# Seven products for eight moved from the down projection to gate and up, in five feed-forward stages

## The chip, the core and the metric
The kernel runs on one core of a Trainium2 chip. A core has TensorE (PE in the profile, its weight loads are PEld), VectorE (DVE), ScalarE (ACT), GpSimd (POOL) and SyncE (SP), which issues the DMAs. Each engine takes its instructions in a fixed order; engines wait for each other through semaphores. The metric is the device time of one execution in microseconds; lower is better.

## What is computed
512 tokens of width 1024 pass through two blocks: a first layer (a state-space mixer beside chunked attention) and four more layers (stick-breaking, differential and convolution mixers). Each of the five layers ends in the same feed-forward stage, which is all that the change touches:

```
h2 = rmsnorm(x, norm_ffn_g[l])
x = x + (jax.nn.silu(h2 @ w_gate[l]) * (h2 @ w_up[l])) @ w_down[l]
```

The hidden width is 2816, which is 22 tiles of 128. Everything is float32.

## The kernel before
Activations lie transposed: `self.x[k]` (k = 0 to 7) holds 128 features by 512 tokens. A float32 product is made of three matmuls in a shorter format: an operand is split by `hilo` (L369, L371) into a high part (ACT copies with rounding) and a low part (DVE subtracts); then hi·hi, hi·lo and lo·hi are added in PSUM (L321, L323, L325). `xh` and `xl` are the parts of the activation times the norm's gain; the norm's factor per token, the tile `bc`, is multiplied in after the product. Weights come by DMA as `raw` tiles of up to eight 128x128 tiles and are split on the way.

The class `Kern` first writes a plan: a list of units (one output tile, up to four k-tiles: 12 matmuls of 512 columns) and of sevenths. `execute` walks the plan; at each item it issues loads, sums and splits two units ahead, then the unit's matmuls, then what follows from the finished product. Generators such as the norm's run a step per item (`tick`). A scheduler below puts the instructions of each engine in their final order by its own forecast of durations.

A group is a block product with four quarters on each side, done by seven products of half the width instead of eight (the Winograd form): GpSimd adds the weights to four sums (L255), the right sides need differences of activations, and the seven results (L272 to L276, matmuls of 256 columns) are added into the output quarters (`take`, L287). Before, gate and up are plain units (`pair`, L526 to L580), and `w_down` is done by groups for 18 of the 22 hidden tiles, in three parts between the units of gate and up; `halves` makes the right sides from the hidden tiles (L637). The last four hidden tiles are plain units at the stage's end. A hidden tile is silu(gate·bc)·bc times up: a multiplication on DVE (L526), silu on ACT (L560), a multiplication on GpSimd (L561), one on DVE (L576).

A PSUM bank of the sevenths comes from `bank`: five rotating "a" banks, or three "z" banks in the layers whose mixers keep them apart.

## Time and profile before

| | us |
|---|---|
| median of 3 runs | 3128.26 |
| lowest, highest | 3126.29, 3129.25 |
| the profiled execution | 3124.52 |
| its span, first to last instruction | 3122.7 |
| PE busy / DVE / ACT / POOL | 3054.8 / 2174.7 / 1502.7 / 1173.0 |

The profile is one execution. A row by line and shape gives the tile written, the tiles read, the form, how often, the busy time, the mean time of one, and how long its engine stood idle just before, with what ended that. A row in time gives the start, the length, the engine, the work. A matmul lasts longer than its step: the next one starts before it ends, so the step between starts is what counts. A stretch counts every instruction that touches it. The five feed-forward stages lie at about 336 to 695, 959 to 1293, 1573 to 1906, 2137 to 2472 and 2756 to 3111 us.

### The profile page before, as it was taken

What the parts mean: (1) busy time and instruction counts of PE and PEld (TensorE: products, weight loads), DVE (VectorE), ACT (ScalarE), POOL (GpSimd) and SP (SyncE); (2) the same over time, 40 slices, a digit from 0 to 9 for tenths busy, and PEclk for the clock granted to TensorE, in tenths of its full rate; (3) what the DMA queues carried; (4) which work ended last, traced back from release to release, by engine and by line L of the source; (5) the groups of instructions that cost most, each with busy time, mean ns of one, the idle gap of its engine ahead of it and who ended that gap; (6) DMA issues with size and microseconds to landing.
All of it is one profiled execution on the core that took longest, in us unless ns stands there. A gap on an engine that the chain in (4) does not pass through costs nothing.

```text
span 3122.7 us, 44415 instructions
## 1 busy us (share of the span) xinstructions
PE 3054.8 (98%) x16236; PEld 2624.9 (84%) x16236; DVE 2174.7 (70%) x3541; ACT 1502.7 (48%) x2793; POOL 1173.0 (38%) x997
## 2 busy tenths in 40 slices
PE   7799999999999999999999999999999999999998
PEld 6687788888887888888878888887888888878887
DVE  8887667677756776766657767655776777567765
ACT  5365444456754444555434435324343567544444
POOL 2731454452314544311145542114444322144543
PEclk9899999999999999999999999999999999999999
DMA  7332333322223333322233332233333322233332
GB/s 240 85 100 78 102 97 92 108 87 68 65 66 120 97 93 106 97 73 73 71 118 102 97 94 93 87 92 118 97 94 101 92 75 62 70 120 92 96 109 66
DMA packets 108203, 295.90 MB, mean 95 GB/s; under 512 B 23216, under 2 KB 27312, under 8 KB 107952
## 3 DMA queue, kind: packets, MB, share of 16 engines
q1 hardware_dynamic: 107984, 293.06, 31.2%
q8 instruction: 128, 2.10, 0.3%
q14 instruction: 91, 0.75, 0.1%
HBM read 286.46 MB, written 6.55 MB: 94 GB/s over the span
## 4 chain that ended last, share of the span: by engine, by line
PE 92%; DVE 4%; POOL 1%; issue 1%; ACT 1%; DMA 1%; SPq 0%; DVEq 0%; POOLq 0%; ACTq 0%
PE g L321 22%; PE g L325 22%; PE g L323 22%; PE a L276 3%; PE a L274 3%; PE a L272 3%; PE z L276 2%; PE z L274 2%; PE z L272 2%; DVE lo L371 1%; PE z L905 1%; PE a L360 1%; PE a L361 1%; DVE x L542 1%; PE a L359 1%
## 5 line engine op out<-in xcount | busy, mean ns | idle before, releaser
L371 DVE TENSOR_TENSOR lo<-raw,hi 128x512 fp32r<-128x512 f32 (+3 forms) x1075 | 862.6, 804 | 335.5 <-ACT hi L369 316.4
L321 PE MATMUL g<-xh,hi 128*128 128x512 f32 x2720 | 1069.7, 393 | 11.7 <-ACT hi L369 7.8
L369 ACT ACTIVATE hi<-raw 128x512 fp32r<-128x512 f32 (+3 forms) x1075 | 638.6, 596 | 903.2 <-PE g L323 694.4
L323 PE MATMUL g<-xl,hi 128*128 128x512 f32 x2720 | 1066.2, 392 | 0.5 <-DVE xl L401 0.5
L325 PE MATMUL g<-xh,lo 128*128 128x512 f32 x2720 | 1062.7, 392 | 0.9 <-DVE lo L371 0.9
L321 PEld LDWEIGHTS g<-xh,hi 128*128 128x128 f32 x2720 | 513.6, 189 | 112.4 <-ACT hi L369 7.8
L325 PEld LDWEIGHTS g<-xh,lo 128*128 128x128 f32 x2720 | 512.4, 188 | 107.4 <-DVE lo L371 1.5
L323 PEld LDWEIGHTS g<-xl,hi 128*128 128x128 f32 x2720 | 513.3, 189 | 97.2 <-DVE xl L401 0.9
L561 POOL TENSOR_TENSOR t<-t,bc 128x512 f32<-128x512 f32 x110 | 151.5, 1379 | 417.4 <-ACT t L560 417.4
L369 ACT ACTIVATE hi<-w 128x384 fp32r<-128x384 f32 x240 | 125.8, 524 | 243.3 <-PE g L323 189.2
L637 POOL TENSOR_TENSOR h<-h 128x256 f32<-128x256 f32 x180 | 177.1, 984 | 162.4 <-DVE h L576 156.9
L371 DVE TENSOR_TENSOR lo<-w,hi 128x384 fp32r<-128x384 f32 x240 | 189.4, 789 | 49.3 <-ACT hi L369 47.9
L421 POOL TENSOR_TENSOR acc<-acc,t 128x512 f32<-128x512 f32 x82 | 117.4, 1438 | 265.3 <-ACT t L420 245.1
L274 PE MATMUL a<-hl,hi 128*128 128x256 f32 x756 | 213.2, 283 | 0.0
L272 PE MATMUL a<-hh,hi 128*128 128x256 f32 x756 | 212.7, 282 | 0.0
L276 PE MATMUL a<-hh,lo 128*128 128x256 f32 x756 | 211.5, 283 | 0.0
L255 POOL TENSOR_TENSOR w<-raw 128x384 f32<-128x384 f32 x120 | 138.1, 1153 | 175.1 <-DMA raw<-in_weights_dram 123.6
L287 POOL TENSOR_TENSOR x<-x,u 128x512 f32<-128x512 f32 x120 | 154.6, 1307 | 111.6 <-DVE u L287 111.6
L526 DVE TENSOR_TENSOR t<-g,bc 128x512 f32<-128x512 f32 x182 | 124.5, 685 | 100.6 <-PE g L325 92.3
L371 DVE TENSOR_TENSOR hl<-h,hh 128x1024 fp32r<-128x1024 f32 x90 | 101.6, 1146 | 69.3 <-ACT hh L369 69.3
L272 PEld LDWEIGHTS a<-hh,hi 128*128 128x128 f32 x756 | 144.6, 191 | 4.5
L274 PEld LDWEIGHTS a<-hl,hi 128*128 128x128 f32 x756 | 144.7, 191 | 4.3
(382 smaller groups left out, 5225.3 us busy)
## 6 DMA issues: line engine op xcount, KB each, us to landing
raw<-in_weights_dram SPq DMA_DIRECT2D x388, 512.0 KB, 3.5
raw<-in_weights_dram SPq DMA_DIRECT2D x131, 384.0 KB, 3.4
raw<-in_weights_dram SPq DMA_DIRECT2D x50, 256.0 KB, 2.7
x<-in_xT_dram SPq DMA_DIRECT2D x16, 256.0 KB, 4.1
raw<-in_weights_dram SPq DMA_DIRECT2D x6, 448.0 KB, 3.3
x<-in_att_bias_dram SPq DMA_DIRECT2D x8, 256.0 KB, 6.0
kv<-kv SPq DMA_DIRECT2D x32, 64.0 KB, 2.3
out_dram<-x SPq DMA_DIRECT2D x8, 256.0 KB, 2.7
```

The costliest lines, as they stand in the source:

```text
L255: nc.gpsimd.tensor_tensor(out=src[out], in0=src[x], in1=src[y], op=ALU.add)
L272: nc.tensor.matmul(out=u.ps, lhsT=wh, rhs=xh, start=i == 0, stop=False)
L274: nc.tensor.matmul(out=u.ps, lhsT=wh, rhs=xl, start=False, stop=False)
L276: nc.tensor.matmul(out=u.ps, lhsT=wl, rhs=xh, start=False, stop=i == len(g.kps) - 1)
L287: eng.tensor_tensor(out=c, in0=c, in1=t, op=op)
L321: nc.tensor.matmul(out=out, lhsT=wh, rhs=xh, start=u.first and i == 0, stop=False)
L323: nc.tensor.matmul(out=out, lhsT=wh, rhs=xl, start=False, stop=False)
L325: nc.tensor.matmul(out=out, lhsT=wl, rhs=xh, start=False, stop=u.last and i == len(u.ks) - 1)
L369: nc.scalar.activation(out=hi, in_=src, func=ACTF.Copy)
L371: eng.tensor_tensor(out=lo, in0=src, in1=hi.bitcast(F32), op=ALU.subtract)
L561: nc.gpsimd.tensor_tensor(out=tg, in0=tg, in1=self.bc(n), op=ALU.mult)
L637: self.nc.gpsimd.tensor_tensor(out=h[:, out], in0=h[:, x], in1=h[:, y], op=op)
```

## The change
Gate and up go by groups, `w_down` by plain units. The first two hidden tiles (`pair(0)`, `pair(1)`) stay plain for gate and up; the other 20 are ten tile pairs, each with a gate group and an up group whose inner dimension is all eight k-tiles (seven products of four k-tile pairs: 84 matmuls of 256 columns). The right sides, differences of the scaled activations, are the same for all twenty groups of a stage; `rights_gen` makes them once at its start: two scaled copies on ACT, one difference on GpSimd, two on DVE, then both parts, for each of four k-tile pairs. Weight parts are split in tiles of 1024 columns (two products at once) with two buffers. The norm, silu and product work on tile pairs of 1024 columns (`gate_got`, `up_got`). The eight plain `w_down` units of each part are set among the groups of the next, after the second and the sixth product of a group; every one adds into `x` (L606 in the new file, L542 before). The stage ends in 16 plain units for the last six hidden tiles. GpSimd's sums and the scaled copies are held in program order against the scheduler.

```diff
 NFF = FF // P
-FF_PARTS = (6, 6, 6, 4)
+FF_PARTS = ((0, 1), (2, 3), (4, 5), (6, 7), (8, 9, 10))
 HALF = T // 2
-SEVEN = ("11", "w3", "w2", "12", "w1", "22", "w4")
+SEVEN = (("11", "11"), ("12", "21"), ("w2", 2), ("w3", 1), ("22", 3), ("w1", 0), ("w4", "22"))
 SUMS_AHEAD = 6
+DOWN_AHEAD = 8
+DOWN_BUFS = 1
+SEVEN_BUFS = 2
 MEM = 256
...
+                    fill(downs[di], self.p_ffn.tile([P, 4 * P], F32, tag="raw", name="raw", bufs=DOWN_BUFS))
+                    di += 1
+                while gi < len(groups) and groups[gi].first <= ui + SUMS_AHEAD and (
+                    (gi < 2 or groups[gi - 2].begun == 5) and (gi < 1 or groups[gi - 1].begun >= 2)
+                ) and all(c.raw is not None for c in groups[gi].chunks):
                     self.sums(groups[gi])
...
-        g.src = src
+        nc, n = self.nc, 4 * P
+        c1, c2 = (c.raw for c in g.chunks)
+        t = [self.p_ffn.tile([P, 2 * n], F32, tag=f"w{i}", name="w", bufs=1 + i) for i in range(2)]
+        (w2, w3), (w1, w4) = ((x[:, :n], x[:, n:]) for x in t)
+        for out, x, y in ((w1, c2[:, :n], c2[:, n:]), (w2, c1[:, :n], w1), (w3, c1[:, :n], c2[:, :n]),
+                          (w4, c1[:, n:], w2)):
+            self.tc.keep_in_program_order(nc.gpsimd.tensor_tensor(out=out, in0=x, in1=y, op=ALU.add))
+        for c in g.chunks:
+            c.left -= 1
+        g.src = {0: c1, 2: t[0], 5: t[1], 4: c2[:, n:]}
...
+        g, n = u.group, 4 * P
+        if u.i not in g.src:
+            u.hi, u.lo = g.next
+            return
+        if u.i == 4:
+            u.hi = self.p_hi.tile([P, n], F32R, tag="hi", name="hi")
+            u.lo = self.p_hi.tile([P, n], F32R, tag="lo", name="lo")
+            self.hilo(u.hi, u.lo, g.src[4])
+        else:
+            hi = self.p_ffn.tile([P, 2 * n], F32R, tag="wh", name="wh", bufs=SEVEN_BUFS)
+            lo = self.p_ffn.tile([P, 2 * n], F32R, tag="wl", name="wl", bufs=SEVEN_BUFS)
+            self.hilo(hi, lo, g.src[u.i])
+            u.hi, u.lo = hi[:, :n], lo[:, :n]
+            g.next = hi[:, n:], lo[:, n:]
+            g.begun = u.i
+        if u.i in (0, 4):
+            g.chunks[u.i == 4].left -= 1
...
+            g.ps = self.bank(self.drawn, [P, 2, HALF])
+        ps = g.ps[:, u.i % 2]
+        for kp in range(KD // 2):
+            wh, wl = u.hi[:, kp * P:(kp + 1) * P], u.lo[:, kp * P:(kp + 1) * P]
+            xh, xl = g.rights(kp, SEVEN[u.i][1])
+            nc.tensor.matmul(out=ps, lhsT=wh, rhs=xh, start=kp == 0, stop=False)
             self.tick(self.fine)
...
+        def tt(out, x, y, op=ALU.add):
+            nc.vector.tensor_tensor(out=out, in0=x, in1=y, op=op)
+        if u.i == 1:
+            g.t = self.p_ffn.tile([P, 2, HALF], F32, tag="u", name="u")
+            g.c = self.p_ffn.tile([P, 2, 2, HALF], F32, tag=g.tag, name=g.tag, bufs=2)
+            nc.scalar.activation(out=g.t[:, 0], in_=ps[:, 0], func=ACTF.Copy)
+            tt(g.c[:, 0, 0], ps[:, 1], g.t[:, 0])
         elif u.i == 3:
-            add(V, c11, ps)
-        elif u.i == 4:
-            add(V, c22, ps, ALU.subtract)
-            add(V, c12, ps)
-        else:
-            add(V, c21 if u.i == 5 else c12, ps)
+            tt(g.t[:, 1], g.t[:, 0], ps[:, 0], ALU.subtract)
+            tt(g.t[:, 0], ps[:, 1], g.t[:, 1], ALU.subtract)
+        elif u.i == 5:
+            tt(g.c[:, 1], ps, g.t[:, 0].unsqueeze(1).to_broadcast([P, 2, HALF]))
+            tt(g.t[:, 1], g.t[:, 1], ps[:, 1], ALU.subtract)
+        elif u.i == 6:
+            tt(g.c[:, 0, 1], ps[:, 0], g.t[:, 1])
+            g.post(g.c.rearrange("p a b c -> p a (b c)"))
...
+    def rights_gen(self, gain):
+        nc = self.nc
+        self.q, t, q = [], {}, {}
+        def sums_of_two(kp):
+            t[kp] = self.p_ffn.tile([P, 4, HALF], F32, tag="cg", name="cg", bufs=2)
+            for e in range(2):
+                k = 2 * kp + e
+                self.tc.keep_in_program_order(nc.scalar.activation(
+                    out=t[kp][:, 2 * e:2 * e + 2].rearrange("p a b -> p (a b)"), in_=self.x[k],
+                    func=ACTF.Copy, scale=gain(k),
+                ))
+            q[kp] = self.p_ffn.tile([P, 4, HALF], F32, tag="cu", name="cu", bufs=2)
+            nc.gpsimd.tensor_tensor(
+                out=q[kp][:, 0:2], in0=t[kp][:, 1].unsqueeze(1).to_broadcast([P, 2, HALF]),
+                in1=t[kp][:, 0:4:3], op=ALU.subtract,
+            )
+        def other_sums(kp):
+            for i, x in ((2, 0), (3, 2)):
+                nc.vector.tensor_tensor(
+                    out=q[kp][:, i], in0=t[kp][:, x], in1=q[kp][:, i - 1], op=ALU.subtract
+                )
+        def in_parts(kp):
+            self.q.append([
+                self.p_ffn.tile([P, 4, HALF], F32R, tag=f"q{c}{kp}", name="q") for c in "hl"
+            ])
+            self.hilo(*self.q[-1], q[kp])
+        n = KD // 2
+        yield
+        for step in range(n + 2):
+            yield
+            for late, do in ((2, in_parts), (1, other_sums), (0, sums_of_two)):
+                if 0 <= step - late < n:
+                    do(step - late)
+    def rights(self, kp, name):
+        if isinstance(name, int):
+            return [t[:, name] for t in self.q[kp]]
+        k, c = 2 * kp + (name[0] == "2"), name[1] == "2"
+        return [t[:, c * HALF:(c + 1) * HALF] for t in self.xg(k)]
...
+        def both(norm):
+            return self.bc(norm).unsqueeze(1).to_broadcast([P, 2, T])
+        def gate_got(kp, c):
+            nc, n = self.nc, norm_of()
+            nc.vector.tensor_tensor(out=c, in0=c, in1=both(n), op=ALU.mult)
+            nc.scalar.activation(out=c, in_=c, func=ACTF.Silu)
+            nc.gpsimd.tensor_tensor(out=c, in0=c, in1=both(n), op=ALU.mult)
+            gates[kp] = c
+        def up_got(kp, c):
+            self.nc.vector.tensor_tensor(out=c, in0=c, in1=gates[kp], op=ALU.mult)
+            self.hilo(*hidden(kp), c)
+        def down(m, part, last):
...
+            for kp in pairs:
+                if kp == 0:
+                    continue
+                for (mat, m), tag, got in ((gate, "cg", gate_got), (up, "cu", up_got)):
+                    g = Group(self.rights, mat, m + 2 * kp, tag, lambda c, got=got, kp=kp: got(kp, c))
+                    sevenths += [Seventh(g, i) for i in range(7)]
+            downs = []
+            if p:
+                for m in range(KD):
+                    u = Unit(down(m, p - 1, False), tiles(FF_PARTS[p - 1]), True, True)
+                    u.down = True
+                    downs.append(u)
+            n = len(sevenths)
+            spots = (list(range(1, n, 7)) + list(range(5, n, 7)))[:len(downs)]
+            for i, u in enumerate(sevenths):
                 self.plan.append(u)
-                self.plan += sevenths[len(sevenths) * i // steps:len(sevenths) * (i + 1) // steps]
-            self.plan += late + sevenths[len(sevenths) * len(mid) // steps:]
-            groups = [
...
+        self.units(outs[:3], (last[:4], last[4:]), 3)
+        self.units(outs[3:], (last[:4], last[4:]))
         self.call(es.close)
```

Where the order of the engines changes, three places are shown. The first is ACT at the start of layer 0's feed-forward stage in the second block, from the norm's factor `bc` on; `hi` and `wh` are weight parts, `hh` hidden parts, `cg` a scaled copy, `q` a right side. Before:

```order
L453 ACTIVATE bc_9532<-a_9527 128x512
L369 ACTIVATE hi_9626<-raw_9512 128x512
L560 ACT_TABLE_LOAD
L560 ACTIVATE t_9568<-t_9568 128x512
L560 ACTIVATE t_9644<-t_9644 128x512
L369 ACTIVATE hi_9659<-raw_9554 128x512
L369 ACTIVATE hi_9676<-raw_9554 128x512
L369 ACTIVATE hh_9653<-h_9572 128x1024
```

In the changed kernel (line numbers are those of the new file):

```order
L433 ACTIVATE wh_9931<-w_9790 128x1024
L517 ACTIVATE bc_9761<-a_9756 128x512
L633 ACT_TABLE_LOAD
L633 ACTIVATE t_9808<-t_9808 128x512
L433 ACTIVATE hi_10098<-raw_9886 128x512
L433 ACTIVATE wh_9989<-w_9791 128x1024
L433 ACTIVATE hh_9814<-t_9812 128x512
L337 ACTIVATE cg_9820<-x2_94,gains_81 128x512
L337 ACTIVATE cg_9820<-x3_95,gains_81 128x512
L337 ACTIVATE cg_9848<-x4_96,gains_81 128x512
L337 ACTIVATE cg_9848<-x5_97,gains_81 128x512
L633 ACTIVATE t_9919<-t_9919 128x512
```

Behind the table load and the silu there stand now the hidden part `hh` and then the scaled copies for the second and third k-tile pair, in front of which nothing of those pairs' right sides can begin.

The second is TensorE at the same place. Before, behind the four transposes that spread the norm's factor:

```order
L449 MATMUL a_9527<-ident_83,rt_9506 128x128 x4
L321 MATMUL g_9578<-xh6_106,hi_9550 128x512
L323 MATMUL g_9578<-xl6_114,hi_9550 128x512
L325 MATMUL g_9578<-xh6_106,lo_9551 128x512
L321 MATMUL g_9578<-xh7_107,hi_9550 128x512
L323 MATMUL g_9578<-xl7_115,hi_9550 128x512
```

In the changed kernel, behind those transposes, 36 matmuls of 512 columns and 24 of 256:

```order
L296 MATMUL z_9976<-q_9842,wh_9931 128x256
L298 MATMUL z_9976<-q_9843,wh_9931 128x256
L300 MATMUL z_9976<-q_9842,wl_9932 128x256
L296 MATMUL z_10007<-q_9842,hi_9970 128x256
L298 MATMUL z_10007<-q_9843,hi_9970 128x256
L300 MATMUL z_10007<-q_9842,lo_9971 128x256
L385 MATMUL g_10226<-hh_9814,hi_10187 128x512
L387 MATMUL g_10226<-hl_9815,hi_10187 128x512
L389 MATMUL g_10226<-hh_9814,lo_10188 128x512
L296 MATMUL z_9976<-q_9871,wh_9931 128x256
L296 MATMUL z_10007<-q_9871,hi_9970 128x256
L298 MATMUL z_9976<-q_9872,wh_9931 128x256
```

Products three to six (`z_9976`, `z_10007`) go forward k-tile pair by k-tile pair, each step naming the next `q` tile, with a piece of a `w_down` unit (`hh`, `hl`) between.

The third is VectorE in the midst of the first block's feed-forward stage. Before, weight parts (`lo`), results taken into `x` and `u`, hidden tiles:

```order
L371 TENSOR_TENSOR lo_5096<-w2_4959,hi_5095 128x384
L371 TENSOR_TENSOR lo_5111<-raw_4847,hi_5110 128x384
L287 TENSOR_TENSOR x2_94<-x2_94,a_5082 128x256
L287 TENSOR_TENSOR x3_95<-x3_95,a_5099 128x512
L371 TENSOR_TENSOR lo_5128<-raw_4830,hi_5127 128x512
L371 TENSOR_TENSOR hl_5073<-h_4869,hh_5072 128x1024
L371 TENSOR_TENSOR hl_5073<-h_4869,hh_5072 128x768
L371 TENSOR_TENSOR lo_5155<-w1_4957,hi_5154 128x384
L287 TENSOR_TENSOR u_5092<-u_5092,a_5133 128x256
```

In the changed kernel, nearly one group (gate's end, then an up group):

```order
L435 TENSOR_TENSOR wl_6283<-w_6158,wh_6282 128x1024
L655 TENSOR_TENSOR cg_6153<-cg_6153,bc_3313 128x1024
L606 TENSOR_TENSOR x5_97<-x5_97,g_6310 128x512
L435 TENSOR_TENSOR wl_6344<-w_6159,wh_6343 128x1024
L308 TENSOR_TENSOR cu_6299<-a_6269,u_6298 128x256
L435 TENSOR_TENSOR lo_6560<-raw_6450,hi_6559 128x512
L308 TENSOR_TENSOR u_6298<-u_6298,a_6330 128x256
L308 TENSOR_TENSOR u_6298<-a_6330,u_6298 128x256
L435 TENSOR_TENSOR wl_6375<-raw_6182,wh_6374 128x1024
L308 TENSOR_TENSOR cu_6299<-a_6361,u_6298 128x512
L308 TENSOR_TENSOR u_6298<-u_6298,a_6361 128x256
L308 TENSOR_TENSOR cu_6299<-a_6394,u_6298 128x256
```

Weight parts are now mostly of 1024 columns, and so are the products with `bc`; the results go to `cg`, `cu` and `u`.

## Rows read from the trace of the kernel before

**Rows 1.** The page: span, busy us (share) xinstructions, the chain's shares by engine.
```profile
span 3122.7 us, 44415 instructions
...
PE 3054.8 (98%) x16236; PEld 2624.9 (84%) x16236; DVE 2174.7 (70%) x3541; ACT 1502.7 (48%) x2793; POOL 1173.0 (38%) x997
...
PE 92%; DVE 4%; POOL 1%; issue 1%; ACT 1%; DMA 1%; SPq 0%; DVEq 0%; POOLq 0%; ACTq 0%
```

**Rows 2.** Stretches: length, then PE, PEld, DVE, ACT, POOL busy (xinstructions), PEclk, DMA.
```profile
978.00:1290.00 312.00, 312.00 (x1731) 273.21 (x1730) 217.24 (x325) 127.72 (x219) 141.34 (x121) 1.00 0.31 92
570.00:604.00 34.00, 34.00 (x151) 28.14 (x151) 20.42 (x28) 13.36 (x20) 11.84 (x11) 1.00 0.38 112
656.00:664.00 8.00, 8.00 (x69) 8.00 (x68) 7.41 (x17) 4.83 (x10) 2.53 (x2) 1.00 0.00 1
```

**Rows 3.** Groups by line and shape, whole span: busy us, mean ns of one, idle before.
```profile
L321 PE MATMUL g<-xh,hi 128*128 128x512 f32 x2720 | 1069.7, 393 | 11.7 <-ACT hi L369 7.8 <-DVE t L526 2.9 <-DVE t L528 0.5
...
L272 PE MATMUL a<-hh,hi 128*128 128x256 f32 x756 | 212.7, 282 | 0.0
...
L371 DVE TENSOR_TENSOR lo<-raw,hi 128x512 fp32r<-128x512 f32 x811 | 679.7, 840 | 228.5 <-ACT hi L369 214.4 <-PE g L325 8.3 <-PE a L449 4.0
...
L371 DVE TENSOR_TENSOR hl<-h,hh 128x1024 fp32r<-128x1024 f32 x45 | 60.5, 1344 | 69.3 <-ACT hh L369 69.3
...
L287 DVE TENSOR_TENSOR x<-x,a 128x256 f32<-128x256 f32 x216 | 85.7, 410 | 0.9
...
L576 DVE TENSOR_TENSOR h<-g,t 128x512 f32<-128x512 f32 x90 | 62.2, 691 | 104.4 <-PE g L325 93.2 <-POOL t L561 11.1
...
L369 ACT ACTIVATE hh<-h 128x1024 fp32r<-128x1024 f32 x45 | 47.8, 1062 | 83.3 <-POOL h L637 83.3
...
L400 ACT ACTIVATE xh<-x,gains 128x512 fp32r<-128x512 f32 x72 | 51.5, 719 | 40.3 <-DVE x L542 40.0 <-DVE cu L1059 0.3
...
L255 POOL TENSOR_TENSOR w<-raw,w 128x384 f32<-128x384 f32 x120 | 146.1, 1219 | 5.6
```

**Rows 4.** GpSimd, then VectorE, near 360 us in time: start, length, work, [idle before].
```profile
364.00 1.30 POOL L561 TENSOR_TENSOR t<-t,bc 128x512 f32<-128x512 f32 x1 [4.34 <-ACT t L560]
...
359.97 1.23 DVE L371 TENSOR_TENSOR hl<-h,hh 128x1024 fp32r<-128x1024 f32 x1 [2.54 <-ACT hh L369]
...
363.18 0.68 DVE L371 TENSOR_TENSOR lo<-raw,hi 128x512 fp32r<-128x512 f32 x1
364.71 1.13 DVE L371 TENSOR_TENSOR lo<-raw,hi 128x512 fp32r<-128x512 f32 x1 [0.85 <-ACT hi L369]
```

**Rows 5.** Low halves of the hidden tiles on VectorE, 390 to 702 us: min/median/max ns.
```profile
L371 DVE TENSOR_TENSOR hl<-h,hh x14: 943/1088/1755, 403.5 to 596.8; 128x1024 fp32r<-128x1024 f32 x7, 128x768 fp32r<-128x768 f32 x7
```

**Rows 6.** Second block, layer 0, start of the feed-forward stage in time: four engines.
```profile
958.40 0.75 DVE L401 SCALAR_TENSOR_TENSOR xl<-x,gains,xh 128x512 fp32r<-128x512 f32 x1 [0.19 <-ACT xh L400]
...
964.14 0.95 PE L438 MATMUL a<-ones,acc 128*128 128x2 f32 x8
...
972.11 0.60 PE L449 MATMUL a<-ident,rt 128*128 128x128 f32 x4
...
972.75 0.60 ACT L453 ACTIVATE bc<-a 128x512 f32<-128x512 f32 x1 [1.39 <-PE a L449]
...
974.56 1.28 ACT L560 ACT_TABLE_LOAD   x1
...
976.56 2.54 POOL L561 TENSOR_TENSOR t<-t,bc 128x512 f32<-128x512 f32 x2 [5.12 <-ACT t L560]
```

**Rows 7.** TensorE's waits, 335 to 356 us, then 690 to 702 us: total, times, longest.
```profile
PE g L321 <- DVE t L526: 1.5, 1, 1.5
PE a L449 <- POOL rt L457: 0.8, 1, 0.8
...
PE a L438 <- POOL acc L421: 0.7, 1, 0.7
```

**Rows 8.** The stretch behind the first two waits of Rows 7, columns as Rows 2.
```profile
349.70:353.20 3.50, 3.50 (x10) 2.73 (x9) 0.69 (x1) 0.57 (x2) 3.21 (x3) 0.51 0.02 8
```

More of the change, by code (lines that the diff above doesn't have):

```diff
@@ L121, in __init__ @@
         self.group, self.i = group, i
-        self.hi = self.lo = self.ps = None
+        self.hi = self.lo = None
 class Chunk:
     def __init__(self, at):
-        self.at, self.tiles, self.left, self.raw = at, 0, 0, None
+        self.at, self.tiles, self.left, self.raw, self.first = at, 0, 0, None, 0
 class Kern:
@@ L181, in execute @@
             at += n
[L182 removed]
+        ci = si = ui = gi = di = 0
         self.drawn = -1
@@ L194, in load @@
             )
+        def load():
+            nonlocal ci
+            fill(chunks[ci], self.p_raw.tile([P, CHUNK * P], F32, tag="raw", name="raw"))
             ci += 1
@@ L265, in mm_seventh @@
     def mm_seventh(self, u):
         nc, g = self.nc, u.group
-        self.drawn += 1
-        u.ps = self.bank(self.drawn, [P, T])[:, :HALF]
-        for i, kp in enumerate(g.kps):
-            wh, wl = u.hi[:, i * P:(i + 1) * P], u.lo[:, i * P:(i + 1) * P]
-            xh, xl = (t[:, u.i] for t in g.hid[kp])
-            nc.tensor.matmul(out=u.ps, lhsT=wh, rhs=xh, start=i == 0, stop=False)
+        if u.i % 2 == 0:
+            self.drawn += 1
+            g.ps = self.bank(self.drawn, [P, 2, HALF])
@@ L542, in add_x, with ffn, hidden @@
         self.nc.vector.tensor_tensor(out=self.x[m], in0=self.x[m], in1=ps, op=ALU.add)
-    def ffn(self, gate, up, down_w, norm_of, after, halves=None):
-        hid, whole = {}, {}
+    def ffn(self, gate, up, down_w, norm_of, after, gain, halves=None):
+        hid, parts, gates = {}, {}, {}
         es = ExitStack()
-        final = NFF - FF_PARTS[-1]
         def begin():
             self.p_ffn = es.enter_context(self.tc.tile_pool(name="ffn", bufs=1))
+            self.rights_of = self.spawn(self.rights_gen(gain))
+        def hidden(kp):
+            parts[kp] = [
+                self.p_ffn.tile([P, 2, T], F32R, tag=tag, name=tag, bufs=4) for tag in ("hh", "hl")
+            ]
+            for e in range(2):
+                hid[2 * kp + e] = [t[:, e] for t in parts[kp]]
+            return parts[kp]
         def up_post(j, st):
@@ L589, in pair @@
             ]
-            self.units(outs, HALVES, 2 if inter else 1)
-        self.call(begin)
-        j, groups = 0, []
-        for part, n in enumerate(FF_PARTS):
-            at = len(self.plan)
-            for jj in range(j, j + n):
-                pair(jj, jj == 0)
-            more, self.plan[at:] = self.plan[at:], []
-            self.plan += more[:4]
-            mid, late = (more[4:-8], more[-8:]) if j + n < NFF else (more[4:], [])
-            sevenths = [Seventh(g, i) for g in groups for i in range(7)]
-            steps = len(mid) + (0 if late else 4)
-            for i, u in enumerate(mid):
-                self.plan.append(u)
-                self.plan += sevenths[len(sevenths) * i // steps:len(sevenths) * (i + 1) // steps]
-            self.plan += late + sevenths[len(sevenths) * len(mid) // steps:]
-            groups = [
-                Group(hid, down_w, m, range(j // 2, (j + n) // 2)) for m in range(0, KD, 2)
-            ]
-            j += n
@@ L614, in out @@
-        def out(m):
-            return Out(hid.__getitem__, down_w, m, lambda ps: after(m, ps, True))
+            self.units(outs, HALVES, 2 if j == 0 else 1)
+        def both(norm):
[6 more added lines that the diff above has]
+            gates[kp] = c
@@ new lines, in up_got, with tiles @@
+        def up_got(kp, c):
+            self.nc.vector.tensor_tensor(out=c, in0=c, in1=gates[kp], op=ALU.mult)
+            self.hilo(*hidden(kp), c)
+        def down(m, part, last):
+            return Out(hid.__getitem__, down_w, m, lambda ps: after(m, ps, last))
+        def tiles(pairs):
+            return [2 * kp + e for kp in pairs for e in range(2)]
+        self.call(begin)
+        pair(0)
+        pair(1)
+        self.call(lambda: self.finish(self.rights_of))
+        for p, pairs in enumerate(FF_PARTS):
+            sevenths = []
+            for kp in pairs:
[13 more added lines that the diff above has]
+            for i, u in enumerate(sevenths):
+                self.plan.append(u)
+                if i in spots:
+                    self.plan.append(downs.pop(0))
@@ L617, in half_out @@
+        last = tiles(FF_PARTS[-1])
+        outs = [down(m, len(FF_PARTS) - 1, True) for m in range(KD)]
         def half_out(c):
@@ L620, in half_out @@
             )
[L622 to L641 removed]
+        if halves is not None:
+            outs = outs[:-1] + [half_out(slice(h, h + HALF)) for h in (0, HALF)]
+        self.units(outs[:3], (last[:4], last[4:]), 3)
+        self.units(outs[3:], (last[:4], last[4:]))
+        self.call(es.close)
     def setup(self, es):
```

141 lines of the change are left out of this document (38 added, 103 removed).

## The prediction, made before the changed kernel was run

> **What bounds the kernel now.** I read the page first: TensorE is busy 98% of the span, DVE 70%, POOL 38%, and the chain that ended last is 92% TensorE [rows 1]. Then one stretch inside a feed-forward stage, 978 to 1290 us: TensorE busy all 312.0 us at granted clock 1.00, DVE 217.2 (70%), POOL 141.3 (45%) [rows 2]. There the time is the number of matmuls times their step, and the other engines count only where they make TensorE wait. So the change has two questions: how much matmul time goes, and where the other engines, which get more to do, come late.
>
> The step comes from counts. In 34.0 us of nothing but 512-column matmuls 151 touch the stretch, in 8.0 us of 256-column ones 69 [rows 2]; with one length (0.39 and 0.28 us [rows 3]) added for those that began before it, the step is 34.39/151 = 0.228 and 8.28/69 = 0.120 us. An edge can shift a count by one, so I take 0.227 and 0.120. Half the columns cost 53% of the step.
>
> **TensorE.** A stage had 384 weight tiles by 512 columns (352 for gate and up, 32 for the last four hidden tiles), times three: 1152 matmuls, and 12 groups x 7 x 3 x 3 = 756 of 256 columns. It gets 32 + 176 = 208 tiles, 624 matmuls of 512, and 20 groups x 7 x 4 x 3 = 1680 of 256. Gone: 528 x 0.227 = 119.9. Added: 924 x 0.120 = 110.9. That is 9.0 us per stage, **45.0** over five.
>
> **DVE inside the groups.** A low part lasts 0.68 us for 512 columns and 1.23 for 1024 while POOL stands idle; one of 512 that began inside a POOL multiplication lasted 1.13 [rows 4], and the longest of 1024 took 1.76 [rows 5]. So 0.5 us is the price of meeting POOL. Operations that read PSUM show none of it: 0.41 for 256 columns, 0.69 for 512 [rows 3]. The means, 0.84 and 1.34 [rows 3], lie a third and a fifth of the way up. A group with one w_down unit beside it costs DVE three weight parts of 1024, one of 512, five results of 256 columns and one of 512, half of three 1024-wide steps (norm, product, hidden low part: one each for a gate and an up group together), and the unit's weight part and addition: 3 x 1.23 + 0.68 + 5 x 0.41 + 0.69 + 1.84 + 0.68 + 0.69 = 10.3 alone, and with 0.53 on each 1024 and 0.5 on each 512 that reads SBUF only, 13.7. TensorE has 84 x 0.120 + 12 x 0.227 = 12.8. At two fifths of the way (POOL is fuller, see below) DVE takes 11.7, 91%. With two units a group it is 13.1 of 15.5. Going through the DVE order of such a group with these times, each weight part is ready some 2.5 us before its product. So I price the steady part at 3 us over the kernel for late weight parts and for the passage from one part of the plan to the next, with 0 and 10 as ends.
>
> **The start of a stage** is where I see a new wait. Products three to six need the right sides, and ACT's order puts the scaled copies of the second to fourth k-tile pair behind the silu chain of the first hidden tile. From the end of `bc`: table load 1.28 [rows 6], silu 0.63 (half of the 1024-wide 1.06 and a little [rows 3]), POOL's multiplication 1.30 [rows 4], the product 0.69, the hidden high part 0.63, two scaled copies of 0.72 [rows 3], POOL's difference of 512 columns 1.3 as the multiplication: 7.3, and some 0.1 at each of seven handovers, 7.9. Then DVE has, in its order and up to the last right side's low part, six subtractions of 256 (0.41, or 0.91 meeting POOL; by the 1.07 ns per column between 0.68 and 1.23), two parts of 512, four of 1024, two PSUM results of 0.69 and 0.41, and it waits 1.06 for ACT's last high part: 10.9 alone, 17.0 always meeting POOL, 13.4 at two fifths. In the meantime TensorE has, behind the four transposes that give `bc`, 36 x 0.227 + 24 x 0.120 before the first right side and 32 x 0.120 + 6 x 0.227 up to the last: 16.2 us; `bc` ends 0.64 us behind the transposes [rows 6], so 15.6 are left. `bc` itself can come later than that, since ACT has the 1024-wide high part of w2 and w3 queued in front of it and that waits for three POOL sums (1.22 for 384 columns [rows 3]); the norm's sum stood 5.0 us behind the last `xl` in the trace and the transposes 13.0 [rows 6], now about two less; I take 1 us late, 0 to 2. The wait is 1 + 7.9 + 13.4 - 15.6 = **6.7** us, ends 2.6 (no handovers, all alone) and 11.3. Queued behind the waiting matmul on TensorE is everything else: its queue goes in order, and what other work there was has been set in front. Four stages: 26.8.
>
> In the first block's stage 24 of the 36 are left after the transposes plus 5, so TensorE has 14.0 us and waits 8.3. But the trace has waits there already, 0.8 for `rt` and 1.5 for a bank [rows 7], and then 3.5 us at clock 0.51, the lower level of 1.2 GHz, in which 10 matmuls ran where 15 fit [rows 8]: 1.6 more. `rt` now stands behind one POOL sum instead of six, and the later waits are inside the new one. Net 8.3 - 3.9 = +4.4 (0.6 to 9).
>
> Behind this the second group's first weight part can only begin when products three and four have ended and freed its buffer: 1.06 on ACT and 1.23 on DVE against about 1.9 us of TensorE's work. I put 0.5 per stage, 2.5 (0 to 5).
>
> **What else moves.** POOL: 80 sums of 512 (for 48 of 384), ten multiplications of 1024, four differences, no more `halves` and no additions into `x`: about 7 us in a group of 12.8, and the next sums have a whole group's time. DMA: the same weights, in 512 and 256 KB pieces; a w_down unit has a single buffer, but its next load has 7 us. Both cost nothing as long as that cover holds; a late load would show as a wait on ACT's `hi`. The end of a stage: up's last hidden parts take 0.41 + 1.23 + 1.06 + 1.23 and some handovers, against 36 matmuls, 8.2 us, so nothing. The last w_down outputs come every 4.1 us instead of 2.7, which takes away the 0.7 us wait for POOL's squares behind the first block's stage [rows 7].
>
> **Sum.** -45.0 + 26.8 + 4.4 + 2.5 + 3 - 0.7 = -9.0 us. Against the profiled execution (3124.5, its span 3122.7) this gives 3115.5; the median of the runs is 3.7 above that execution, so **3119**. With all lower ends it is 3128.3 - 33.5 = 3095, with all upper ones 3128.3 + 24 = 3152.
>
> **Rivals.**
> 1. The starts are hidden: TensorE waits under 3 us in each. For it: if `bc` comes on time and POOL hardly meets DVE, my chain gives 2.6. Against: the chain of seven handovers in a fixed order leaves nothing to shorten it, and POOL is nearly always busy there. Then 5 x 0 to 2.6 on -45 and the small terms: 3083 to 3098, say 3090.
> 2. DVE becomes the bound inside the groups, and the kernel is slower. With POOL met each time a one-unit group is 13.7 against 12.8 and a group without a unit 11.8 against 10.1: four of the first kind and two of the second per stage make 7 us, 35 in all: 3119 + 35 = 3154. It decides from the point where (12.8 - 10.3)/3.4 = three quarters of the parts meet POOL. Against: a third does so now. For: POOL's operations get longer.
> The Trainium skill ("SBUF — State Buffer", "Who interferes with whom") says that a DVE instruction with two SBUF inputs and a GpSimd instruction that reads SBUF exclude each other for the whole of the one that came first. By that a 1024-wide multiplication on POOL, some 2.6 us as an estimate from twice the 1.30, could hold a weight part for all of it, where the trace, with nothing on POOL over 512 columns, never shows over 0.53 on a 1024 part: ten times up to 2 us more per stage, which would eat the margin of the gate groups.
> 3. The waits at the start take the clock down. In the first block two waits of 0.8 and 1.5 were followed by 3.5 us at 0.51 [rows 8], a loss of 1.6. If each of the five new waits does that: 3119 + 8 = 3127, no change. Against: the new wait comes in pieces, with matmuls in between.
> The Trainium skill ("TensorE: Matmul & The Clock Gate", "What's actually happening") has the clock fall after idleness, whatever caused it; the row agrees, and the price is the row's.
>
> **Chances.** My forecast 0.50 (own range 3100 to 3135), rival 1 0.15, rival 2 0.22, rival 3 0.13. A measurement of this kernel can tell about 0.2%, 6.3 us, from no change, so faster means under 3122.0 and slower over 3134.5. Faster: 0.31 of the forecast, all of rival 1, 0.03 of rival 3: 0.49. Slower: nearly all of rival 2 and 0.06 of the forecast and of rival 3: 0.26. Same: 0.25. The range 3090 to 3152 leaves out half of rival 1 and half of rival 2.
>
> **What the profile would show.** In the five stages 3120 matmuls of 512 columns (2640 fewer) and 8400 of 256 (4620 more), still at steps of 0.227 and 0.120. TensorE's waits: five clusters, one behind each `bc`, for the right sides (`q`, ended by DVE or ACT), 5 to 9 us each; little else inside a stage. DVE near 90% in the last part of a stage. I am wrong if the waits at the starts add up to under 13 or over 50 us, if `wl` waits run through whole stages (rival 2), or if 256-column matmuls take other steps with `q` and `wh` than with hidden tiles: each nanosecond there is worth 4.6 us over the 4620 added.

## The result and the profile after

The changed kernel takes 3224.11 us (3215.48 to 3228.75), 1.031 times the 3128.76 of the kernel before, run beside it [1.0298, 1.0323]: 95 us slower, outside the range of the prediction. Its profiled execution took 3221.08, span 3219.0. The page (busy us and share by engine, then the chain that ended last by engine):

```profile
span 3219.0 us, 47660 instructions
...
PE 3055.3 (95%) x18222; PEld 2705.2 (84%) x18222; DVE 2467.8 (77%) x3512; ACT 1503.9 (47%) x2574; POOL 1311.8 (41%) x827
...
PE 23%; POOL 7%; issue 5%; DVE 4%; DMA 3%; ACT 1%; SPq 0%; DVEq 0%; POOLq 0%; ACTq 0%
```

The shares of this chain add up to 43% of the span only: it can be followed back no further than to 1836 us, where its first piece stands:

```profile
1836.38 5.01 issue
```

Of these 43% TensorE has 23, about half, where it had 92% of the whole in [rows 1]; GpSimd, "issue" and DMA came in, so in that part the end is no longer set by matmuls alone. TensorE's busy time doesn't show what was saved (3055.3 against 3054.8), in part because matmuls at the lower clock last longer.

To divide the time I took, for each pair of neighbouring matmuls in the trace, the time between their starts less the usual step of their shape (0.227 and 0.120 us, as before). These excesses add up to 95.7 us before and 236.9 after, 141.2 more. The span grew by 96.3, so matmul time fell by 44.9; the prediction had 45.0. Everything that went wrong is waits, and slow clock behind waits. In the table, of the five stages added up, a "start" reaches from 10 us ahead of the silu table load to 35 behind it, and an "end" is the last 75 us of a stage. Losses by the slow clock are included. Where exactly a stage is taken to end moves the last two columns by 2 or 3 us. The experiments ran in sets, each with the kernel before beside it; its medians, 3124.5 to 3128.8, show that times of different sets compare to some 4 us:

| kernel | starts | middle | ends | median us |
|---|---|---|---|---|
| before | 8.9 | 0.0 | 2.6 | 3124.5 to 3128.8 |
| changed | 81.2 | 47.1 | 22.0 | 3224.1 |
| e1 no sums | 47.4 | 0.0 | 2.1 | 3119.4 |
| e2 dead sums | 74.5 | 27.6 | 8.8 | 3180.9 |
| e3 one w_down load | 79.1 | 0.0 | 10.1 | 3158.0 |
| e4 no right sides | 21.4 | 34.8 | 17.4 | 3140.1 |
| e5 second pair plain | 25.3 | 45.6 | 10.2 | 3156.4 |
| e6 three buffers | 96.1 | 1.0 | 9.4 | 3173.6 |
| e7 both | 19.5 | 16.3 | 8.5 | 3120.0 |
| e8 first w_down later | 17.6 | 3.6 | 9.0 | 3106.5 |
| e9 all w_down later | 17.7 | 5.8 | 7.1 | 3109.0 |
| e10 both marks off | 36.4 | 6.8 | 1.8 | 3121.1 |
| e11 rights earlier | 80.1 | 40.3 | 17.5 | 3206.4 |
| e12 sums' mark off | 76.0 | 6.3 | 1.8 | 3152.0 |
| e13 copies' mark off | 30.9 | 41.0 | 16.6 | 3161.0 |
| e14 e8, copies' mark off | 17.4 | 0.0 | 7.8 | 3102.1 |
| e15 e8, both marks off | 19.1 | 0.0 | 2.1 | 3097.9 |

**The middle of a stage.** The stretch of [rows 2] in the changed kernel, and one of 250 us inside the second stage (columns as there), then TensorE's and ScalarE's waits in the latter (total, times, longest):

```profile
978.00:1290.00 312.00, 296.25 (x1994) 273.44 (x1994) 256.73 (x296) 123.97 (x167) 170.44 (x93) 0.98 0.32 95
1030.00:1280.00 250.00, 243.92 (x1700) 228.69 (x1699) 211.22 (x244) 93.86 (x125) 139.12 (x72) 0.99 0.34 99
```
```profile
PE z L296 <- ACT wh L433: 4.6, 2, 3.7
PE z L300 <- DVE wl L435: 1.5, 1, 1.5
```
```profile
ACT hi L433 <- DMA raw<-in_weights_dram: 76.0, 13, 11.5
```

VectorE is busy 84% there (211.2 of 250), not full. But ScalarE stands idle for 76 us waiting for loads. What such a wait costs is seen at one of them, in time, on GpSimd, VectorE, SyncE, ScalarE and TensorE:

```profile
1089.14 2.41 POOL L657 TENSOR_TENSOR cg<-cg,bc 128x1024 f32<-128x1024 f32 x1 [8.92 <-ACT cg L656]
1091.50 2.30 POOL L262 TENSOR_TENSOR w<-raw 128x512 f32<-128x512 f32 x1
1093.88 1.62 POOL L262 TENSOR_TENSOR w<-raw,w 128x512 f32<-128x512 f32 x1
1095.46 2.27 POOL L262 TENSOR_TENSOR w<-raw 128x512 f32<-128x512 f32 x1
...
1096.50 1.77 DVE L435 TENSOR_TENSOR lo<-raw,hi 128x512 fp32r<-128x512 f32 x1
...
1097.76 2.51 SPq L201 DMA_DIRECT2D raw<-in_weights_dram  x3
...
1105.39 0.63 ACT L433 ACTIVATE hi<-raw 128x512 fp32r<-128x512 f32 x1 [11.49 <-DMA raw<-in_weights_dram]
1105.92 1.04 ACT L433 ACTIVATE wh<-w 128x1024 fp32r<-128x1024 f32 x1
...
1107.02 0.39 PE L296 MATMUL z<-q,wh 128*128 128x256 f32 x1 [3.66 <-ACT wh L433]
```

GpSimd's order has the gate multiplication ahead of the next group's first sum, so it idles 8.92 us for a silu. That silu (`cg` on ScalarE, at 1088.02) had itself stood behind a weight copy that waited for an earlier load, so the lateness feeds itself:

```profile
1087.48 0.63 ACT L433 ACTIVATE hi<-raw 128x512 fp32r<-128x512 f32 x1 [3.40 <-DMA raw<-in_weights_dram]
```

The third sum ends at 1097.7 and frees a buffer; at 1097.76 SyncE can issue the load for it, and behind that another and the w_down unit's. The w_down load is the third of these. Its own single buffer comes free at 1098.27, when the low part of the unit before (`lo` at 1096.50) is done; so the single buffer and the place in the queue both make it late. ScalarE's `hi` for it starts at 1105.39, after 11.49 us of idling. The group's own `wh`, whose sum was long done, stands behind `hi` in ScalarE's order, and TensorE waits 3.66 us for it.

**The starts.** The second stage's: the stretch (columns as above), TensorE's two largest waits in it, then ScalarE and VectorE in time; [rows 6] is the same place before:

```profile
995.00:1030.00 35.00, 26.30 (x147) 22.22 (x146) 26.82 (x30) 18.42 (x25) 14.95 (x11) 0.85 0.24 76
```
```profile
PE z L298 <- DVE q L435: 4.3, 2, 3.5
PE g L389 <- DVE lo L435: 3.0, 1, 3.0
```
```profile
996.56 0.58 ACT L517 ACTIVATE bc<-a 128x512 f32<-128x512 f32 x1
...
1007.98 1.06 ACT L433 ACTIVATE q<-cu 128x1024 fp32r<-128x1024 f32 x1 [2.12 <-DVE cu L349]
...
1016.12 1.06 ACT L433 ACTIVATE q<-cu 128x1024 fp32r<-128x1024 f32 x1 [0.53 <-DVE cu L349]
...
1019.74 1.06 ACT L433 ACTIVATE q<-cu 128x1024 fp32r<-128x1024 f32 x1 [2.57 <-DVE cu L349]
```
```profile
996.69 1.23 DVE L435 TENSOR_TENSOR wl<-w,wh 128x1024 fp32r<-128x1024 f32 x1 [2.28 <-ACT wh L433]
...
1005.00 2.88 DVE L349 TENSOR_TENSOR cu<-cg,cu 128x256 f32<-128x256 f32 x2 [1.91 <-POOL cu L342]
1007.81 1.75 DVE L435 TENSOR_TENSOR lo<-raw,hi 128x512 fp32r<-128x512 f32 x1
1009.48 2.30 DVE L435 TENSOR_TENSOR wl<-w,wh 128x1024 fp32r<-128x1024 f32 x1
1011.71 1.48 DVE L349 TENSOR_TENSOR cu<-cg,cu 128x256 f32<-128x256 f32 x1
...
1018.77 0.41 DVE L349 TENSOR_TENSOR cu<-cg,cu 128x256 f32<-128x256 f32 x1
```

The second to fourth right sides come 11, 20 and 23 us behind `bc`, as the prediction's chain has it, but several VectorE steps take two to three and a half times their time alone: a subtraction of 256 columns 1.48 us against 0.41, a low part of 1024 columns 2.30 against 1.23. TensorE's wait of 3.0 us is not for a right side but for the low part of a w_down unit's weights (`lo` at 1007.81), which stands behind two of those subtractions in VectorE's order. The granted clock of the stretch is 0.85: after idling in this wait TensorE ran for some 10 us at its lower level, 1.2 GHz (0.51 between 1009 and 1019 us):

```profile
1009.00:1019.00 10.00, 5.63 (x19) 4.45 (x20) 9.90 (x10) 3.22 (x6) 6.52 (x5) 0.51 0.27 79
```

GpSimd works without a gap beside those VectorE steps:

```profile
1007.56 1.45 POOL L262 TENSOR_TENSOR w<-raw 128x512 f32<-128x512 f32 x1
1009.09 1.61 POOL L262 TENSOR_TENSOR w<-raw,w 128x512 f32<-128x512 f32 x1
1010.66 2.24 POOL L262 TENSOR_TENSOR w<-raw 128x512 f32<-128x512 f32 x1
```

Over the kernel 183 of the 300 `wl` overlap a GpSimd operation; their median is 2.30 us, that of the others 1.22.

### The profile page after: what moved, and what is told of

Read it like the earlier page. It is cut to its first block, busy times and chain, and to the rows that moved or that the text cites. A ratio compares the mean times of both kernels' runs of the same rounds, so it can differ in the third digit from the quotient of the medians.

```text
span 3219.0 us, 47660 instructions
## 1 busy us (share of the span) xinstructions
PE 3055.3 (95%) x18222; PEld 2705.2 (84%) x18222; DVE 2467.8 (77%) x3512; ACT 1503.9 (47%) x2574; POOL 1311.8 (41%) x827
## 5 line engine op out<-in xcount | busy, mean ns | idle before, releaser
L385 PE MATMUL g<-xh,hi 128*128 128x512 f32 x1120 | 443.5, 396 | 12.0 <-ACT hi L433 7.8
L389 PE MATMUL g<-xh,lo 128*128 128x512 f32 x1120 | 440.8, 394 | 0.9 <-DVE lo L435 0.9
L262 POOL TENSOR_TENSOR w<-raw 128x512 f32<-128x512 f32 x200 | 394.3, 1971 | 113.5 <-DMA raw<-in_weights_dram 112.0
L387 PE MATMUL g<-xl,hi 128*128 128x512 f32 x1120 | 440.1, 393 | 0.0
L262 POOL TENSOR_TENSOR w<-raw,w 128x512 f32<-128x512 f32 x200 | 356.7, 1783 | 143.8 <-issue 137.7
L435 DVE TENSOR_TENSOR wl<-w,wh 128x1024 fp32r<-128x1024 f32 x200 | 363.9, 1819 | 64.2 <-ACT wh L433 61.8
L389 PE MATMUL g<-hh,lo 128*128 128x512 f32 (+1 forms) x886 | 346.4, 391 | 12.5 <-DVE lo L435 12.5
L387 PE MATMUL g<-hl,hi 128*128 128x512 f32 (+1 forms) x886 | 347.5, 392 | 3.0 <-DVE hl L435 3.0
L385 PE MATMUL g<-hh,hi 128*128 128x512 f32 (+1 forms) x886 | 345.5, 394 | 3.8 <-ACT hi L433 3.5
L296 PE MATMUL a<-q,wh 128*128 128x256 f32 x720 | 207.9, 289 | 28.6 <-ACT wh L433 27.3
L298 PE MATMUL a<-q,wh 128*128 128x256 f32 x720 | 207.2, 288 | 1.2 <-DVE q L435 1.1
```

The source lines that it names most:

```text
L262: self.tc.keep_in_program_order(nc.gpsimd.tensor_tensor(out=out, in0=x, in1=y, op=ALU.add))
L296: nc.tensor.matmul(out=ps, lhsT=wh, rhs=xh, start=kp == 0, stop=False)
L298: nc.tensor.matmul(out=ps, lhsT=wh, rhs=xl, start=False, stop=False)
L385: nc.tensor.matmul(out=out, lhsT=wh, rhs=xh, start=u.first and i == 0, stop=False)
L387: nc.tensor.matmul(out=out, lhsT=wh, rhs=xl, start=False, stop=False)
L389: nc.tensor.matmul(out=out, lhsT=wl, rhs=xh, start=False, stop=u.last and i == len(u.ks) - 1)
```

## The experiments

Three theories run through the expectations. A: VectorE and GpSimd shut each other out, so weight parts come late. B: a late load in the queue holds ScalarE, and with it the parts behind. C: the starts wait for the chain that makes the right sides. All waits below are in us, by the places of the table.

**e1 and e2: the sums left out, and made for nobody.** In both, `g.src` gives a tile of constants, `wc`, in place of the sums. e1 makes no additions; in e2 GpSimd adds the halves of `wc` four times per group into a tile that nobody reads:

```
-            self.tc.keep_in_program_order(nc.gpsimd.tensor_tensor(out=out, in0=x, in1=y, op=ALU.add))
...
-        g.src = {0: c1, 2: t[0], 5: t[1], 4: c2[:, n:]}
+        g.src = {0: c1, 2: self.wc, 5: self.wc, 4: c2[:, n:]}
```

> The four weight sums per group on GpSimd are left out; products two to four, six and seven split a tile of constants of the same size instead, so VectorE, ScalarE and TensorE do as much as in the changed kernel and only GpSimd does less. In the changed kernel's trace TensorE waits about 65 us more than before inside the five stages and about 74 us more at their starts. Theory A (VectorE and GpSimd shut each other out, so the operations of both get longer and weight parts come late) and theory B (the sums and the w_down loads come late one behind the other in the load queue, contention matters little) both expect the 65 us to go: about 3160, or 3145 if the 12 us wait for a sum at the start of the third stage goes too. A expects the low part of 1024 columns to fall from a mean of 1.82 us to under 1.4. If neither holds and the waits are VectorE's own amount of work, the time stays over 3200.

> GpSimd makes as many additions of 512 columns as in the changed kernel, but on a tile of constants and into a tile that nobody reads; the products split constants as in the run without sums. So the contention stays and nothing waits for the sums. Theory A expects low parts of 1024 columns to stay near 1.8 us and at least half of the 65 us inside the stages to stay: 3180 to 3220. Theory B expects the waits gone as without sums: about 3145 to 3160, within 10 us of that run.

e1: 3119.38, well below both forecasts: the waits in the middle and at the ends are gone, and the starts, which neither theory had moved, are down to 47.4. Low parts of constants take a mean of 1.50 us, so A's mark of 1.4 was just missed. e2: 3180.88, low parts at 1.79. So additions that nobody waits for cost 61.5 us: 27.6 in the middle, 27.1 at the starts, 6.7 at the ends. Half of the 69 us behind the starts stay, which is theory A's mark, and B's 3145 to 3160 was missed; what the real sums add to that, 43 us, comes from what waits for them. But e2 doesn't show that contention alone makes the 61.5 us. Its additions are held in GpSimd's order too, among the gate multiplications that the hidden tiles need. TensorE's waits for a hidden tile's low part, 3.0 us in the changed kernel, are

```profile
PE g L386 <- DVE hl L434: 8.7, 9, 2.0
```

and ScalarE still waits 276 us for loads over the whole kernel (440 in the changed one). Contention, held order and late loads aren't taken apart by this run.

**e3: one w_down load per stage.** `downs[di].raw` is the first load's tile for all units among the groups.

> The w_down units among the groups all split the weights of the stage's first such load; the other 31 loads per stage of 256 KB are left out, the sums and all else stay. Theory B (ScalarE's weight copy waits at the head of its queue for the w_down load, behind which the group's own weight parts stand) expects the 65 us inside the stages to fall to under 20: about 3165 to 3175. Theory A expects at least 40 of them to stay: over 3200. The starts should not move.

3157.98. The middle falls from 47.1 to 0.0 us, though `wl` still takes a mean of 1.63 us over the kernel (1.71 in the changed one). Theory B holds there: with the contention nearly as before and no late loads, nobody waits in the middle; it takes the late load at the head of ScalarE's queue. The 10 us left are at the ends, where groups have one w_down unit and TensorE waits for `wl`.

**e4: no right sides.** `rights` gives halves of `xh` and `xl`; `rights_gen` does nothing.

> The right sides are not made: products three to six take the halves of the scaled activations that are there anyway. Sums, loads and all groups stay. Theory C (the chain of scaled copies, differences, subtractions and parts is what the starts wait for) expects the 74 us at the five starts to fall to under 20: 3165 or less. Its rival (the starts wait for the sums and weight parts, which GpSimd and VectorE make late anyway) expects at least 40 of them to stay: 3185 or more. Waits inside the stages should stay at about 65.

3140.13, the starts at 21.4 (a little over the 20 put): 60 of the 72 us that the change had added there come from the chain, by what it makes late itself and by what stands behind it on VectorE and GpSimd. The waits behind the starts, expected to stay, fell from 69 to 52.

**e5 to e7: more TensorE work ahead of the right sides, more buffers for w_down, and both.**

```
-        pair(0)
-        pair(1)
+        for j in range(4):
+            pair(j)
...
-DOWN_BUFS = 1
+DOWN_BUFS = 3
```

> The second tile pair of each stage goes by plain units too: 18 groups for 20, and 21.8 us of TensorE's work more between bc and the first product that needs a right side, for 20.2 of groups less. Matmul time + 1.6 us a stage, 8 in all. Theory C (the starts wait for the chain of right sides, which runs on beside any work that TensorE has) expects the waits at the starts to fall from 81 us to about 25 and a tenth of the 69 inside the stages to go with the two groups: 3224 - 56 + 8 - 7 = about 3170. Its rival (the chain stands in the engines' order behind the silu chains of the plain units, so the waits move with it) expects at least 50 of the 81 to stay: 3200 or more.

> Three buffers for the w_down loads, the room taken from the second buffer of up's result and of the differences. All work stays. Theory B (inside the stages the w_down load with its single buffer, queued behind the groups' loads, holds ScalarE's queue) expects the 47 us in the middle of the stages to fall to under 10, as with the loads left out: 3224 - 40 = about 3184, some 5 us more if the right sides suffer from the single buffer. Theory A (contention makes the parts late whatever the loads do) expects at least 30 of the 47 to stay: 3205 or more.

> The second pair plain and three buffers for the w_down loads. If the two causes are separate, the gains add: 3224 - 56 + 8 - 47 = about 3130, at or a little above the kernel before, with waits of some 25 us at the starts and 15 at the ends of the stages. If both are faces of one cause (VectorE and GpSimd are full), the second gives little: 3160 or more.

e5: 3156.37 and starts of 25.3, as theory C said (a little better, since the ends gained 12 where 7 were put for all). e6: 3173.61, middle 1.0; the starts got worse by 15, where I had put 5 for the single buffer. e7: 3120.01, 0.9982 [0.9973, 0.9992]: the causes are separate in the main, 10 us better than put. Against the changed kernel e5 and e6 gain 67.7 and 50.5 us, together 118; e7 gains 104, and the 14 that are missing are about the 16.3 in its middle.

**e8 and e9: w_down units later.** In e7 one wait of 3 us per stage is left, for the last plain tile's hidden part:

```profile
PE g L385 <- ACT hh L433: 2.9, 1, 2.9
```
```
-            spots = (list(range(1, n, 7)) + list(range(5, n, 7)))[:len(downs)]
+            spots = (list(range(3 if p == 1 else 1, n, 7)) + list(range(5, n, 7)))[:len(downs)]
```

> As the run with both remedies, and in the first part that has groups the w_down units stand behind the fourth product of a group for the second (the other one behind the sixth, as it was). In the run with both, the one large wait left per stage is 3.0 to 3.7 us for the last plain hidden tile's high part, which a w_down unit needs 3 us too early, and behind it the clock falls for 1.4 to 2.7 us. Theory: both go, 5 x (3.2 + 2.3) = 27 us: about 3093. Rival: the wait only goes to the next thing that comes late (a weight part, a right side): 3110 or more.

> The same for all parts: w_down units behind the fourth and the sixth product of a group. If the waits of 1 to 2 us for low parts near the end of each stage come from the second product's place, which follows a whole weight part on VectorE, another 5 us go: about 3088. If they come from VectorE's amount of work in groups with one w_down unit, nothing more goes: within 5 us of the run before; if spacing matters, a few us worse.

e8: 3106.48, 13.5 us of the 27. The clock losses behind the wait went (the middle fell from 16.3 to 3.6), but of the wait itself most came back at the next late thing, as the rival had it: the starts fell by 1.9 only, and in the second stage TensorE now waits, for a right side,

```profile
PE z L298 <- DVE q L435: 2.3, 1, 2.3
```

e9, which has `range(3, n, 7)` for all parts: 3108.97, no difference from e8; the ends don't hang on the place of a unit.

**e10 to e13: the two marks of program order taken off, both and one by one, and the right sides one unit earlier.**

```
-            self.tc.keep_in_program_order(nc.gpsimd.tensor_tensor(out=out, in0=x, in1=y, op=ALU.add))
+            nc.gpsimd.tensor_tensor(out=out, in0=x, in1=y, op=ALU.add)
```

The mark on the scaled copies, ScalarE's activations in `rights_gen`, goes in the same way; e11 leaves out the first `yield` of `rights_gen` and keeps both marks.

> The changed kernel without the two marks that keep GpSimd's sums and the scaled copies in program order; nothing else. If the order of the right sides is what makes the starts late, the starts' 81 us of waits fall to under 60: 3200 or less. If the chain's length and the contention make them, the time stays within 15 us of 3224.

> The changed kernel with the right sides made one unit earlier; nothing else. The chain's first links (scaled copies) then stand one unit, 2.7 us, earlier in the order. If the chain binds the starts as a whole, each start gains up to 2.7 us, 13 in all: about 3211. If the silu chain and the contention of the weight parts hold it, less than 5 us either way.

> The changed kernel; only the mark on GpSimd's sums is taken off, the scaled copies stay in program order. Freeing both gave 3121: 45 us less at the starts, 54 inside and at the ends of the stages. If the two marks act apart, the sums' one answers for the 54 inside (waits in the middle and at the ends under 15) and the starts stay near 81: 3224 - 54 = about 3170. If the sums' order is what makes the starts late too, 3130 or less.

> The changed kernel; only the mark on the scaled copies is taken off, the sums stay in program order. If the two marks act apart, the starts fall from 81 to about 36 and the 69 us behind them stay: 3224 - 45 = about 3179. If the sums' order holds the starts, 3210 or more.

e10: 3121.12 with all work and every buffer as in the changed kernel. This was the surprise: 103 us hang on the order. e12 (3152.04) has the middle and ends at 8.1 us and the starts at 76; e13 (3161.00) the starts at 30.9 and the rest at 57.6. In the main the marks act apart: the sums' one makes what is lost behind the starts, the copies' one the late right sides. Not wholly, though: the gains of e12 and e13, 72 and 63 us, make 135, and both marks together give 103. VectorE and GpSimd remain contended: in e10 `wl<-w,wh` takes a mean of 1.81 us, as in the changed kernel (1.82). GpSimd in e12, at the place shown above:

```profile
1091.90 1.29 POOL L262 TENSOR_TENSOR w<-raw 128x512 f32<-128x512 f32 x1 [4.42 <-DMA raw<-in_weights_dram]
1097.10 2.40 POOL L657 TENSOR_TENSOR cg<-cg,bc 128x1024 f32<-128x1024 f32 x1 [3.91 <-DVE wl L435]
```

The first sum goes ahead of the gate multiplication as soon as its load lands, and ScalarE's waits for loads, 76.0 us in the 250 shown above, come to less in a stretch of 240 us:

```profile
ACT hi L433 <- DMA raw<-in_weights_dram: 48.3, 12, 6.5
```

Over the whole kernel they fall from 440 to 257 us, still many, while TensorE's excess in the middle falls from 47.1 to 6.3. So their sum is not what counts: a weight part that TensorE needs at once has to stand behind one, as at the place above.

In e10 ScalarE makes the last right side before `bc`, which they don't need:

```profile
974.20 1.06 ACT L433 ACTIVATE q<-cu 128x1024 fp32r<-128x1024 f32 x1 [4.71 <-DVE cu L349]
975.17 1.04 ACT L433 ACTIVATE wh<-w 128x1024 fp32r<-128x1024 f32 x1
976.11 0.58 ACT L517 ACTIVATE bc<-a 128x512 f32<-128x512 f32 x1
```

e11: 3206.37, 18 us better, but the starts hardly moved (80.1; the first stage's gained 7, the second and the fifth lost 3 each), and the middle and the ends gained 11. Neither expectation had that, and its cause stays open.

**e14 and e15: e8 with the copies' mark off, and with both.**

> The run with the second pair plain, three buffers and the first w_down units later (3106), with the scaled copies out of program order. What is left there is 17.6 us of waits at the starts and 9 at the ends. If the copies' place makes what is left at the starts, up to 10 us go: 3096; if those waits are the norm's and the silu chain's own, within 5 us of 3106.

> The same with both marks off. The free order took the waits at the ends from 19 to 2 and in the middle from 47 to 7: if it does the same here, the ends' 9 us go as well: about 3090 to 3098. The first block's mixer waited 7 us longer with both marks off; if the free order costs that here and gives nothing, 3106 to 3113.

e14: 3102.14, 0.9924 [0.9912, 0.9937], within 5 us of e8, which runs of different sets can't tell apart. The starts are at 17.4 against 17.6 in sum, less in three stages and more in the first and third: no 10 us hang on the copies' place. e15: 3097.87, 0.9911 [0.9897, 0.9924], the fastest by its median and as put: middle 0.0, ends 2.1. Its second stage, 345 us of it and TensorE's only wait there:

```profile
960.00:1305.00 345.00, 344.26 (x2234) 315.22 (x2233) 276.91 (x342) 149.72 (x206) 169.89 (x96) 1.00 0.34 100
```
```profile
PE g L385 <- DVE t L590: 0.7, 1, 0.7
```

## Why the prediction was wrong

**TensorE: right.** -45.0 forecast, -44.9 measured; steps 0.227 and 0.120 also with `q` and `wh`. The rest of the 96.3 us by which the span grew is 72.3 at the starts, 66.5 behind them and 2.4 outside the stages.

**"Both cost nothing as long as that cover holds": wrong, and the largest miss.** That "the next sums have a whole group's time" and that "its next load has 7 us" was judged each by itself, and the cost was put at nothing. The cover didn't hold, and the sign named ("a wait on ACT's `hi`") came: 76 us of it in 250. The two are links of one chain (sum, buffer, queue of loads, single w_down buffer, ScalarE's order), and the term for the "steady part", 3 us, should have been 47 + 19 = 66. e3, e6 and e12 each break one link and all but empty the middle (0.0, 1.0 and 6.3).

**The start: the right cause, but the path and the size were wrong.** 31.2 net (26.8 + 4.4) against 72.3. e4 gives the chain's share, 60. The prediction has TensorE wait for the right sides themselves, "5 to 9 us each". But of the 51 us that TensorE idles in the five starts only 11 end with a `q`; 12.5 end with a w_down unit's `lo`, which stands behind the subtractions on VectorE, and 12.9 with the `wh` of the third start below. The path to the last right side, which was priced, was not the only one through VectorE's order.

Two terms were short besides. The price of meeting GpSimd, 0.5 us, was read from [rows 4, 5], where meetings were brief; it measured 1.1 at the median of `wl`. The row of 512 columns could have been read otherwise: its GpSimd multiplication ends 0.59 us after the low part of 512 columns began, and that low part took 1.13 us in place of 0.68, so the 0.5 was about what was left of the multiplication and not a price of its own. The sentence on the Trainium skill ("SBUF — State Buffer", "Who interferes with whom") said that such a pair holds each other off for the whole of the first operation. The trace now agrees: 0.41 + 1.07 = 1.48 for 256 columns, beside GpSimd operations of 1.29 alone. And the chain was taken as behind `bc` by necessity: e10 and e13, with starts of 36.4 and 30.9, show that the copies' held place put it there. The order rows ahead of the prediction show it; I priced the place and did not ask whose choice it was.

**Rival 2 (VectorE the bound, 35 us)** did not come true, though the ends looked like it: 22.0 us of waits, of which 9.4 stay when the loads are cured (e6). With the sums' mark off these go too (1.8 in e12), and there VectorE has as much work as in the changed kernel. **Rival 3 (clock)** came true in mechanism: the slow stretches behind waits cost 21.4 us in the stages against 1.8 before, where 8 were put; more waits, more stretches. One was at the third start, where TensorE waited 11.9 us at once for a `wh` whose sums stood among the right sides' differences in GpSimd's order, and whose copy then stood behind a `q` on ScalarE:

```profile
PE a L296 <- ACT wh L433: 12.9, 2, 11.9
```

No rival had the load queue, so none came near 3224.

One sum of the working is off, and nothing hangs on it: the lower ends add up to -34.7, not -33.5.

What stays open: how much of the 61.5 us of e2 is contention and would be left with the marks off. No run has dead sums in free order; e15, where `wl<-w,wh` still takes a mean of 1.77 us and the stages have 21 us of waits, speaks for little.

## What to carry to other kernels

An instruction held in program order holds back what stands behind it in its engine's queue, here 103 us of 3224: before pricing a change that fixes an order, follow each held instruction to the buffer it frees and the queue that waits for that buffer. That each engine has time enough is no cover when three engines' queues are linked through single buffers. And a price of contention read from brief meetings was too low here: 0.5 us read, 1.1 measured.

## What the hardware showed that I had not expected

A VectorE operation of two SBUF inputs that begins inside a GpSimd one pays what is left of the other, less a little: `wl` takes 1.22 us alone and up to 2.83 in the changed kernel. In 173 of the 181 cases where GpSimd had begun first, `wl` ended 1.08 to 1.10 us after GpSimd's operation, that is 0.12 to 0.14 less than its own 1.22. In the two cases where `wl` had begun first it took 1.22. All 21 subtractions of 256 columns that met GpSimd in this way ended so too, 0.12 to 0.14 us less than their own 0.41 after it. GpSimd pays too: its sums of 512 columns took 1.97 and 1.78 us in the mean against 1.29 alone.

```profile
L262 POOL TENSOR_TENSOR w<-raw 128x512 f32<-128x512 f32 x200 | 394.3, 1971 | 113.5 <-DMA raw<-in_weights_dram 112.0 <-DVE u L308 1.5
L262 POOL TENSOR_TENSOR w<-raw,w 128x512 f32<-128x512 f32 x200 | 356.7, 1783 | 143.8 <-issue 137.7 <-DVE wl L435 1.2
L435 DVE TENSOR_TENSOR wl<-w,wh 128x1024 fp32r<-128x1024 f32 x200 | 363.9, 1819 | 64.2 <-ACT wh L433 61.8 <-PE g L387 2.4
```
